# An expert layer whose results are collected with tokens on partitions, on top of the residual, and a final norm that reads them there

## The chip, the cores and the metric

One core of a Trainium2 chip runs the whole program. The metric is the device time of one execution in microseconds: the median of 3 runs, 805.72 us (803.02 to 806.88).

## The reference

A trunk of two layers over 256 tokens of width 1024, all in fp32. Each layer is a mixer and a hierarchical mixture of 16 experts, both behind an RMS norm with a learned shift, scale and gate; a final RMS norm ends it. Cut to the last expert sub-layer and the norm:

```python
hcur = rms_norm(x, norm2_g[layer]) * (1 + sc2) + sh2
for e in range(N_EXPERTS):
    hid = jax.nn.silu(xt @ w_gate[e]) * (xt @ w_up[e])
    y = y + gates[:, e:e + 1] * (hid @ w_down[e])
x = x + g2 * y
return rms_norm(x, final_norm_g)
```

Each token has a gate above zero for two experts only. Widths: 1024 to 512 (gate and up) and 512 to 1024 (down).

## The kernel before, in words

Tensors that lie with features on partitions hold feature n * 8 + k (n the partition, k from 0 to 7) in block k; the residual is `xT`, 128 partitions x 8 blocks x 256 tokens. The tokens of an expert layer are gathered into slots, sorted by expert, and the slots are worked through as 20 tasks of 64 or 32 slots (`_tasks`, lines 66 to 82): 8 tasks of 64 and 12 of 32 a layer. Four (or two) tasks fill a pack of 128 slots; there are 7 packs.

A task is: `first_half` and `second_half` (lines 1473 and 1484: gate and up products, in 2 column groups of TensorE for 64 slots, in 4 for 32 slots), `hidden` (Silu and product), `turn` (transposes), and `project` (line 1493), which calls `down` (line 1381). `down` puts its result with slots on partitions in a PSUM bank; G is 128 / slots, and each of the G column groups makes the part of the features whose k lies in its q = 8 / G blocks. The weights of `down` lie in a buffer of [128, 2048] with features in order n * 8 + k, so its moving operand `src[:, :, q * g:q * (g + 1)]` reads q neighbouring values, then the next n, 8 values further on. `project` then splits the result into a rounded part and a rest (`yp`, lines 1511 and 1512, ScalarE and VectorE, G times each), reordered so that k is outermost. When a pack is full, `combine` (line 1514) adds it to `acc`, four PSUM banks: 16 products of 256 columns, whose moving operand is `ptts`, the 0/1 matrix of slots by tokens, so the sum comes out with features on partitions and tokens in columns. `acc` is started with four zero products (line 1529). All of it runs one task ahead: the halves of task i + 1 stand around the transposes and the `down` of task i (loop at line 1531).

After the last `combine`, eight VectorE steps (line 1563) add gate times `acc` to `xT`. The final norm (lines 1584 to 1630) squares `xT` on ScalarE, sums over features with products against ones (`square_sums`), turns the sums to tokens (`to_tokens`), turns `xT` block by block to tokens on partitions (line 1602; some blocks with a diagonal matrix of the norm's gains, `dg`), takes 1/sqrt as Exp of Ln, scales into `ot` on ScalarE and VectorE, and stores in four transfers of 256 KB.

TensorE and SP (the queue of all loads) run in the order of the program; VectorE and ScalarE do so inside `in_order()`, elsewhere a scheduler orders them. Weights come in pieces of 1 MB in a fixed order (`moe`, line 166: six pieces an expert) into 15 buffers and a few more; SP issues a load as soon as TensorE has emptied a buffer (`pump`, line 261, called from `free`). Which experts the loads fetch is known only after routing, so the stream stops there and starts again. Line 135 is the helper of all products. At task 9 stands a branch for tokens that overflow an expert's slots (`whatever_is_left`, line 1432, with `further` in it); with these inputs it is not taken.

Of the kernel before, what the change touches and what calls it, by code (L numbers as in the profile page):

```python
# [19 lines left out]
P = 128  # L20
# [92 lines left out]
def trunk_kernel(ctx: ExitStack, tc: tile.TileContext, a, out, dbg=None):  # L113
# [20 lines left out]
    def mm(o, l, r, start=False, stop=False):  # L134
        T.matmul(o, l, r, start=start, stop=stop, skip_group_check=True)  # L135
# [1167 lines left out]
    def place(rr, e, base, G):  # L1303

        pe = sb.tile([P, 2, P], BF, name="pe", tag="pt")
# [4 lines left out]
        return pe  # L1310

    def moe_layer(l, before, then):
        table(LEXP)
        if l == 0:
            drain_ada()
# [19 lines left out]
        with in_order():  # L1335
            g3, rr, hs, ofi, exi, pe = route(l, wa, cb, lg, th, tl, sm)

        def load_window(o, base, n, tag=None):
            w = sb.tile([P, KD, n], F32, name="win", tag=tag or "sq", bufs=1 if tag else 3)
            A.copy(w, hs[:, :, ds(o + base, n) if base else ds(o, n)])  # L1340
            return w

        def slots(e, base, pe):
# [8 lines left out]
            ptt = sb.tile([P, S], F32R, name="ptt", tag="rs")  # L1352
            A.copy(ptt, b[:, 0:S])
            return ptt, gs


        def gate_up(w, wts, b, G, halves=(0, 1)):
# [15 lines left out]
        def turn(hid, b, G, tag="ht"):  # L1373
# [3 lines left out]
            ht = sb.tile([P, m, G, P // G], F32, name="ht", tag=tag)  # L1377
            A.copy(ht.rearrange("p c g s -> p (c g s)"), b[:, 0:n])  # L1378
            return ht

        def down(ht, wts, G, bs2=(6,)):

            n, r, m, q = D // G, P // G, DE // G // P, KD // G
            ys = [bank(i) for i in bs2]
            y = [ys[g % len(ys)] for g in range(G)]
            for j in range(4):
                src = k3(wts[j // 2], 2)[:, j % 2, :].rearrange("p (n k) -> p n k", k=KD)
                for g in range(G):
                    mm(y[g][g * r:(g + 1) * r, 0:n], ht[:, j % m, j // m, :], src[:, :, q * g:q * (g + 1)],
                       start=(j == 0), stop=(j == 3))  # L1390
            return y

        def above(e, n):
# [3 lines left out]
        def further(p, base, bk):  # L1397

            def load(name, tag, cut):
                r = sb.tile([P, 2048], F32, name="raw", tag=tag)  # L1400
                e = p if p < FIXED else nc.sync.value_load(exi[0:1, p:p + 1], min_val=0, max_val=NE - 1)
                nc.sync.dma_start(k3(r, 4 if name != "moe_w_down" else 2), cut(a[name][l, e]))
                return r

            tags = ("f8", "m8", "f8", "m8")
            wts = []
            for h in range(2):
                for name in ("moe_w_gate", "moe_w_up"):
                    wts.append(load(name, tags[len(wts)],
                                    lambda w: w.rearrange("(p k) n -> p k n", k=KD)[:, 4 * h:4 * h + 4, :]))  # L1410
                if h == 0:
                    b = bank(bk)
                    pt, gs = slots(p, base, place(rr, p, base, 2))
                    o = nc.scalar.value_load(ofi[0:1, 16 + p:17 + p], min_val=0, max_val=2 * S - base)
                    w = load_window(o, base, 64, "m8b")
                gate_up(w, wts, b, 2, (h,))
            ht = turn(hidden(b, gs, 2, "r8"), b, 2, "m8b")
            wts = [load("moe_w_down", tags[h], lambda w: w.rearrange("(j p) n -> p j n", p=P)[:, 2 * h:2 * h + 2, :])
                   for h in range(2)]
            y = down(ht, wts, 2)[0]  # L1420
            y2 = sb.tile([P, 2, 512], F32R, name="y2", tag="r8")
            A.copy(y2[:, 0, :], y)
            V.tensor_sub(y2[:, 1, :], y, y2[:, 0, :].bitcast(F32))
            for n in range(2):
                yx = y2[:, n, :]
                for kk in range(4):
                    for g in range(2):
                        k, rows = 4 * g + kk, slice(64 * g, 64 * g + 64)
                        mm(acc[k // 2][:, (k % 2) * S:(k % 2 + 1) * S],
                           yx.rearrange("p (n k) -> p k n", k=4)[rows, kk, :], pt[rows, :])  # L1430

        def whatever_is_left(bk):
            left = nc.values_load(ofi[0:1, 32:33], min_val=0, max_val=2 * S)
# [59 lines left out]
        def project(i, ht):  # L1493
            t = TASKS[i]
            p, r, G = t["p"], t["row"], P // t["n"]
            if t["first"]:
                dw_[p] = take_all([("moe_w_down", l, p)] * 2)
            y = down(ht, [w for w, _ in dw_[p]], G, (4 + n % 2, 7) if i == n - 1 else (6,))
            if i == n - 1:
                table(LEXP)  # L1500
            if t["last"]:
# [3 lines left out]
                yy[0] = [sb.tile([P, KD, P], F32R, name="yp", tag=x) for x in ("m4a", "m4b")]  # L1505
            yh, yl = yy[0]
            q, w = KD // G, P // G
            for g in range(G):
                src = y[g][g * w:(g + 1) * w, 0:D // G].rearrange("p (n k) -> p k n", k=q)
                o = slice(r, r + w), slice(q * g, q * (g + 1))  # L1510
# [1 line left out]
                V.tensor_sub(yl[o[0], o[1], :], src, yh[o[0], o[1], :].bitcast(F32))  # L1512

        def combine(j, last=False):
            for x in range(2):
# [5 lines left out]
        yy, ptts = [None], {}  # L1521
# [6 lines left out]
        for a4 in acc:  # L1528
            mm(a4, zero, identb.unsqueeze(1).to_broadcast([P, 4, P]), start=True)
        prepare(1)  # L1530
        for i, t in enumerate(TASKS):
            if i == LEFT:
# [22 lines left out]
                ptts[j] = turned_pack(j)  # L1555
            if st["fin"]:
                ada_flush(7, -1)
        with in_order():
            combine(PACKS - 1, last=True)
            before()  # L1560
            warm(WARM[5])
            for k in (0, 1, 4, 5, 2, 3, 6, 7):
# [15 lines left out]
    dump("x2", xT)  # L1578
    odd_mixer(1)
    dump("x3", xT)  # L1580
    moe_layer(1, lambda: None, lambda: None)
    dump("x4", xT)

    ot = sb.tile([P, 2, D], F32, name="ot", tag="f8")
    ov = ot.rearrange("p t (n k) -> p t k n", k=KD)
    rt = sb.tile([P, 2], F32, name="rt", tag="Rrt")
    fb = sb.tile([P, D], F32, name="fb", tag="r8")
    nc.sync.dma_start(fb, a["final_norm_g"].partition_broadcast(P))
    fv = fb.rearrange("p (n k) -> p k n", k=KD)

    dg = sb.tile([P, 4, P], F32, name="dg", tag="m8b")
    for i, k in enumerate((0, 1, 4, 5)):
        V.tensor_scalar(dg[:, i, :], ident, ng3[:, k:k + 1], None, op0=OP.mult)
    table(LEXP)
    with in_order():
        st2 = bank(0)
        tk = bank(1)
        bk = [bank(4 + i) for i in range(4)]

        def turned(k):  # L1600
            for t in range(2):
                o = bk[k // 2][:, t * S + k % 2 * P:t * S + (k % 2 + 1) * P]
                if k % 4 < 2:
                    mm(o, xT[:, k, t * P:(t + 1) * P], dg[:, k // 4 * 2 + k % 2, :], start=True, stop=True)
                else:
                    T.transpose(o, xT[:, k, t * P:(t + 1) * P], ident)  # L1606

        ks = []
        for _, k in square_sums(st2, 0, 4):
            ks.append(k)  # L1610
            if len(ks) in (3, 5, 7):
                turned(ks[-3])
                turned(ks[-2])
        tk = to_tokens(st2, tk, diag[:, 0:1])
        turned(ks[-2])
        turned(ks[-1])
        A.activation(rt, tk[:, :, 0], AF.Ln, scale=1.0 / D, bias=eps)  # L1617
        A.activation(rt, rt, AF.Exp, scale=-0.5)  # L1618
        for t in range(2):
            for i in range(4):  # L1620
                c = slice(2 * i, 2 * i + 2)
                src = k3(bk[i][:, t * S:(t + 1) * S], 2)
                if i % 2:
                    V.scalar_tensor_tensor(ov[:, t, c, :], src, rt[:, t:t + 1], fv[:, c, :], op0=OP.mult, op1=OP.mult)  # L1624
                else:
                    A.activation(ov[:, t, c, :], src, AF.Copy, scale=rt[:, t:t + 1])
    for tt in range(2):
        for h2 in range(2):
            c = slice(h2 * 512, (h2 + 1) * 512)
            nc.sync.dma_start(out[0, tt * P:(tt + 1) * P, c], ot[:, tt, c])  # L1630


_INS = ["x", "c", "rel_bias", "norm1_g", "norm2_g", "w_ada", "b_ada", "ev_w_in", "ev_w_out",
# [21 lines left out]
```

## Time and profile before

| | us |
|---|---|
| median of 3 runs | 805.72 |
| lowest, highest | 803.02, 806.88 |
| the profiled execution | 803.79 |
| its span in the profile | 802.0 |
| TensorE products busy | 695.3 |
| VectorE, ScalarE busy | 375.4, 236.8 |

Times in the profile are from the start of the span. A row names the line, the operation, the tiles written and read, the shape of one instruction and how many; "PEld" is TensorE's load of a stationary operand, which overlaps its products. An fp32 product appears as two records. The granted clock is 1.00 when TensorE runs at full speed.

### The profile page before, as it was taken

To read this page: it belongs to the slowest core of one execution; us is meant where nothing else is said; L and a number is where in the kernel's file an instruction comes from. 1 tells how busy PE (TensorE), PEld (TensorE's weight loads), DVE (VectorE), ACT (ScalarE), POOL (GpSimd) and SP (SyncE) were. 2 spreads that over 40 slices of the span, in tenths; PEclk is the share of its full clock that TensorE was granted. 3 is DMA by queue.
4 is the path that set the end of the run, shared out by engine and by line. 5 is a ranking of instruction groups with operands and counts; after the bars stand their busy time and mean duration, and the time that the engine had idled before them with its cause. 6 is when DMAs were issued, how large, how long until landed. Compare 5 with 4: busy or idle time off the path is not lost. (4 is left out here: it accounts for less than half of the span.)

```text
span 802.0 us, 18126 instructions
## 1 busy us (share of the span) xinstructions
PE 695.3 (87%) x7589; PEld 478.9 (60%) x7589; DVE 375.4 (47%) x866; ACT 236.8 (30%) x530; POOL 13.2 (2%) x33
## 2 busy tenths in 40 slices
PE   4699899978999959997669989998999995999765
PEld 3376358956666637544338878775666664755433
DVE  2516788877322212211158999997722231221114
ACT  3211143041222213211055326473322221321114
POOL 0010002000000000000000000000000000000000
PEclk9799899999999979999899999999999998999988
DMA  8989999967999999999999999321899999999991
GB/s 300 370 290 402 400 406 409 418 253 300 350 416 412 417 407 407 416 418 415 415 400 397 398 409 409 103 81 54 335 401 415 408 419 392 411 416 413 417 406 66
DMA packets 70029, 288.12 MB, mean 359 GB/s; under 512 B 8909, under 2 KB 11273, under 8 KB 53544
## 3 DMA queue, kind: packets, MB, share of 16 engines
q1 hardware_dynamic: 69928, 286.77, 90.1%
q8 instruction: 63, 1.03, 0.5%
q14 instruction: 38, 0.31, 0.1%
HBM read 285.69 MB, written 1.06 MB: 358 GB/s over the span
## 5 line engine op out<-in xcount | busy, mean ns | idle before, releaser
L135 PE MATMUL b<-raw,win 128*32 128x128 f32 (+1 forms) x3712 | 198.5, 309 | 36.3 <-DVEq L1434 16.9
L135 PEld LDWEIGHTS b<-raw,win 128*32 128x32 f32 (+1 forms) x3712 | 141.2, 120 | 85.7 <-issue 28.9
L1512 DVE TENSOR_TENSOR yp<-b,yp 32x256 fp32r<-32x256 f32 (+1 forms) x128 | 62.5, 488 | 143.5 <-ACT yp L1511 143.3
L135 PE MATMUL b<-raw,ht 128*32 128x256 f32 (+1 forms) x1024 | 113.5, 460 | 15.1 <-DMA raw<-in_moe_w_down_dram 15.0
L1511 ACT CAST yp<-b 32x256 fp32r<-32x256 f32 (+1 forms) x128 | 53.3, 417 | 131.0 <-PE b L135 93.2
L135 PEld LDWEIGHTS b<-raw,ht 128*32 128x32 f32 (+1 forms) x1024 | 42.1, 119 | 69.8 <-issue 34.5
L319 DVE SCALAR_TENSOR_TENSOR raw<-raw,csil 128x1024 f32<-128x1024 f32 x56 | 74.6, 1332 | 4.3 <-DMA raw<-in_w_ada_dram 3.2
L1370 DVE SCALAR_TENSOR_TENSOR hid<-hid,gs,b 128x128 f32<-128x128 f32 (+1 forms) x40 | 16.0, 401 | 113.4 <-ACT hid L1369 113.4
L914 DVE SCALAR_TENSOR_TENSOR ac<-hqk,dw,ac 128x256 f32<-128x256 f32 x120 | 50.7, 481 | 0.3
L135 PE MATMUL b<-h,raw 128*128 128x256 f32 x192 | 44.8, 392 | 5.3 <-ACT h L584 2.9
L135 PE MATMUL b<-hh,whf 128*128 128x256 f32 x160 | 41.7, 299 | 4.1 <-DVE whf L588 3.7
L135 PEld LDWEIGHTS b<-h,raw 128*128 128x128 f32 x192 | 37.1, 196 | 13.1 <-ACT h L584 3.8
L1369 ACT ACTIVATE hid<-b 128x128 f32<-128x128 f32 (+1 forms) x40 | 12.8, 320 | 105.5 <-PE b L135 105.5
L135 PE MATMUL b<-mx,raw 128*128 128x256 f32 x160 | 40.6, 409 | 0.0
L135 PEld LDWEIGHTS b<-mx,raw 128*128 128x128 f32 x160 | 38.8, 335 | 1.0 <-issue 0.8
L135 PE MATMUL b<-hl,whf 128*128 128x256 f32 x128 | 37.2, 290 | 0.4 <-DVE hl L849 0.4
L1378 ACT COPY ht<-b 128x128 f32<-128x128 f32 (+1 forms) x40 | 12.3, 308 | 84.6 <-PE b L1376 84.5
L1471 DVE TENSOR_REDUCE gs<-b 128x1 f32<-128x3 f32 x40 | 6.4, 161 | 65.9 <-PE b L135 65.5
L135 PE MATMUL b<-ptt,yp 128*128 128x256 f32 x224 | 34.4, 295 | 2.4 <-ACT yp L1511 1.6
L135 PEld LDWEIGHTS b<-hh,whf 128*128 128x128 f32 x160 | 29.7, 200 | 7.5 <-DVE whf L588 4.1
L135 PEld LDWEIGHTS b<-ptt,yp 128*128 128x128 f32 x224 | 28.4, 188 | 9.3 <-ACT yp L1511 6.6
L135 PE MATMUL b<-raw,h 128*128 128x512 f32 x64 | 31.5, 640 | 0.0
(287 smaller groups left out, 825.9 us busy)
## 6 DMA issues: line engine op xcount, KB each, us to landing
raw<-in_moe_w_gate_dram SPq DMA_DIRECT2D x64, 1024.0 KB, 13.1
raw<-in_moe_w_up_dram SPq DMA_DIRECT2D x64, 1024.0 KB, 14.7
raw<-in_moe_w_down_dram SPq DMA_DIRECT2D x64, 1024.0 KB, 16.5
raw<-in_w_ada_dram SPq DMA_DIRECT2D x48, 1024.0 KB, 15.8
raw<-in_ev_w_in_dram SPq DMA_DIRECT2D x10, 1024.0 KB, 13.1
raw<-in_od_w_in_dram SPq DMA_DIRECT2D x10, 1024.0 KB, 18.4
raw<-in_ev_w_out_dram SPq DMA_DIRECT2D x4, 1024.0 KB, 15.0
raw<-in_od_w_out_dram SPq DMA_DIRECT2D x4, 1024.0 KB, 14.0
```

The lines of the kernel that those rows point to most:

```text
L135: T.matmul(o, l, r, start=start, stop=stop, skip_group_check=True)
L319: ins = V.scalar_tensor_tensor(acc, src, csil[:, k:k + 1], acc, op0=OP.mult, op1=OP.add)
L914: V.scalar_tensor_tensor(ac[:, m, :], src, dw[:, m, j:j + 1], ac[:, m, :], op0=OP.mult, op1=OP.add)
L1369: A.activation(hid, b[:, 0:n], AF.Silu)
L1370: V.scalar_tensor_tensor(hid, hid, gs, b[:, n:2 * n], op0=OP.mult, op1=OP.mult)
L1378: A.copy(ht.rearrange("p c g s -> p (c g s)"), b[:, 0:n])
L1471: V.tensor_reduce(gates[i], g, AX.X, OP.add)
L1511: A.copy(yh[o[0], o[1], :], src)
L1512: V.tensor_sub(yl[o[0], o[1], :], src, yh[o[0], o[1], :].bitcast(F32))
```

## The change

`moe_layer` takes a new argument `rows`, true for the second layer alone. There, `down` reads its weights so that its columns come out in order k, n. `project` multiplies the result by the gate row (`gains`), splits it in SBUF and stores the parts by blocks. `combine` swaps its operands: the 0/1 matrix is stationary and the results move, 8 products of 512 columns a pack, and the sum has tokens on partitions. `acc` starts from the residual, turned by 16 plain products against the identity. The gate rows are made at the start of the layer: POOL scales eight identity blocks by the gate (`dg`), and TensorE multiplies them with ones, once for 32-slot and once for 64-slot tasks. The final norm reads `acc` directly: squares on ScalarE for the first 128 tokens, statistics on VectorE for the others, and scaling from the banks into `ot`, a quarter of it over ScalarE and POOL; two stores of 512 KB. The table of final gains (`fb`) is loaded at task 17 of 20. In the branch that is not taken the buffers move to other tiles. The core of the diff:

```diff
-        def down(ht, wts, G, bs2=(6,)):
+        def down(ht, wts, G, bs2=(6,), rows=False):
...
-                    mm(y[g][g * r:(g + 1) * r, 0:n], ht[:, j % m, j // m, :], src[:, :, q * g:q * (g + 1)],
-                       start=(j == 0), stop=(j == 3))
+                    c = src[:, :, q * g:q * (g + 1)]
+                    mm(y[g][g * r:(g + 1) * r, 0:n], ht[:, j % m, j // m, :],
+                       c.rearrange("p n k -> p k n") if rows else c, start=(j == 0), stop=(j == 3))
...
+            bs2 = (6,) if i < n - 1 else (4 + n % 2,) if rows else (4 + n % 2, 7)
+            y = down(ht, [w for w, _ in dw_[p]], G, bs2, rows)
...
+            if rows:
+                ys = sb.tile([P, D // G], F32, name="ys", tag="sq", bufs=3)
+                V.tensor_mul(ys, y[0][:, 0:D // G], gains[G])
+                yr = sb.tile([P, D // G], F32R, name="yr", tag="sq", bufs=3)
+                A.copy(yr, ys)
+                ys2 = ys.bitcast(F32R)
+                rest(ys2, ys, yr)
+                for g in range(G):
+                    o = slice(r, r + w), slice(q * g, q * (g + 1))
+                    A.copy(yh[o[0], o[1], :], k3(yr[g * w:(g + 1) * w, :], q))
+                    V.tensor_copy(yl[o[0], o[1], :], k3(ys2[g * w:(g + 1) * w, :], q))
+                return
...
         def combine(j, last=False):
+            if rows:
+                pt = ptts.pop(j)
+                for t in range(2):
+                    for h in range(2):
+                        for x in range(2):
+                            mm(acc[2 * t + h], pt[:, t * P:(t + 1) * P],
+                               yy[0][x][:, 4 * h:4 * h + 4, :], stop=(last and x == 1))
+                return
...
+        if rows:
+            ada_flush(7, -1)
+            dg = [sb.tile([P, 4, P], F32, name="dg", tag="sq", bufs=3) for _ in range(2)]
+            for k in range(KD):
+                G.tensor_scalar(dg[k // 4][:, k % 4, :], ident, M(l, 5, k), None, op0=OP.mult)
...
+        if rows:
+            for n4, tag in ((4, "pt"), (2, "gr2")):
+                b = bank(6)[:, 0:D // n4]
+                for k in range(KD):
+                    g, kk = k * n4 // KD, k % (KD // n4)
+                    w = P // n4
+                    mm(b[g * w:(g + 1) * w, kk * P:(kk + 1) * P], ones[:, 0:w], dg[k // 4][:, k % 4, :],
+                       start=True, stop=True)
+                gains[n4] = sb.tile([P, D // n4], F32, name="gains", tag=tag)
+                A.copy(gains[n4], b)
+            for t in range(2):
+                for k in range(KD):
+                    mm(acc[2 * t + k // 4][:, k % 4 * P:(k % 4 + 1) * P], xT[:, k, t * P:(t + 1) * P], ident, start=(k % 4 == 0))
+        else:
+            for a4 in acc:
+                mm(a4, zero, identb.unsqueeze(1).to_broadcast([P, 4, P]), start=True)
...
+            if rows and i == n - 3:
+                before()
         with in_order():
             combine(PACKS - 1, last=True)
+            if rows:
+                then(acc)
+                return
...
+    def final_norm(acc):
...
+        for h in range(2):
+            sq = sb.tile([P, 512], F32, name="sq", tag="sq", bufs=3)
+            A.activation(sq, acc[h], AF.Square, accum_out=ss[:, h:h + 1])
+        for h in range(2):
+            V.bn_stats(st6[:, h, :], acc[2 + h])
+        V.tensor_add(rt[:, 0:1], ss[:, 0:1], ss[:, 1:2])
+        A.activation(rt[:, 0:1], rt[:, 0:1], AF.Ln, scale=1.0 / D, bias=eps)
+        A.activation(rt[:, 0:1], rt[:, 0:1], AF.Exp, scale=-0.5)
+        V.bn_aggr(mv, st6)
+        V.scalar_tensor_tensor(rt[:, 1:2], mv[:, 0:1], mv[:, 0:1], mv[:, 1:2], op0=OP.mult, op1=OP.add)
+        A.activation(rt[:, 1:2], rt[:, 1:2], AF.Ln, bias=eps)
+        A.activation(rt[:, 1:2], rt[:, 1:2], AF.Exp, scale=-0.5)
+        sq = sb.tile([P, 512], F32, name="sq", tag="sq", bufs=3)
+        A.activation(sq, acc[1], AF.Copy, scale=rt[:, 0:1])
+        G.tensor_mul(ov[:, 0, 4:8, :], k3(sq, 4), fv[0][:, 4:8, :])
+        for x in (0, 2, 3):
+            c = slice(x % 2 * 4, x % 2 * 4 + 4)
+            V.scalar_tensor_tensor(ov[:, x // 2, c, :], k3(acc[x], 4), rt[:, x // 2:x // 2 + 1], fv[0][:, c, :],
+                                   op0=OP.mult, op1=OP.mult)
+        for t in range(2):
+            nc.sync.dma_start(out[0, t * P:(t + 1) * P, :], ot[:, t, :])
```

## Rows read from the trace of the kernel before

**Rows 1.** The page: TensorE's and the other engines' busy time and share.

```profile
PE 695.3 (87%) x7589; PEld 478.9 (60%) x7589; DVE 375.4 (47%) x866; ACT 236.8 (30%) x530; POOL 13.2 (2%) x33
```

**Rows 2.** Windows: us, busy PE, PEld, DVE, ACT, POOL, granted clock, DMA share, GB/s.

```profile
580.00:600.00 20.00, 20.00 (x380) 12.59 (x378) 5.19 (x15) 5.12 (x14) 0.00 (x0) 1.00 1.01 403
...
740.00:760.00 20.00, 14.16 (x204) 8.50 (x201) 2.37 (x5) 2.25 (x6) 0.00 (x0) 1.00 1.02 414
760.00:780.00 20.00, 13.70 (x186) 7.10 (x186) 2.15 (x5) 2.33 (x6) 0.00 (x0) 0.83 1.02 415
```

**Rows 3.** Waits of TensorE's products, 560 to 802 us: total us, times, longest.

```profile
PE b L135 <- DMA raw<-in_moe_w_down_dram: 7.7, 8, 1.4
PE b L135 <- DMA raw<-in_moe_w_up_dram: 5.0, 7, 1.3
PE b L135 <- DMA raw<-in_moe_w_gate_dram: 3.1, 4, 1.8
```

**Rows 4.** Groups of instructions, whole span: busy us, mean ns of one, idle before.

```profile
L135 PEld LDWEIGHTS b<-h,raw 128*128 128x128 f32 x192 | 37.1, 196 | 13.1 <-ACT h L584 3.8
...
L135 PEld LDWEIGHTS b<-mx,raw 128*128 128x128 f32 x160 | 38.8, 335 | 1.0 <-issue 0.8
...
L677 ACT CAST who<-raw 128x256 fp32r<-128x256 f32 x12 | 8.1, 683 | 6.7 <-PE b L135 6.7
...
L977 ACT CAST mhl<-g 128x256 fp32r<-128x256 f32 x4 | 1.5, 405 | 0.0
```

**Rows 5.** Order of time: two runs of stationary loads, start us, us, count.

```profile
162.74 3.91 PEld L135 LDWEIGHTS b<-mx,raw 128*128 128x128 f32 x16 [0.41 <-issue]
...
789.45 0.97 PEld L135 LDWEIGHTS b<-dg,xT 128*128 128x128 f32 x8 [0.41 <-issue]
```

**Rows 6.** Order of time: products of expert tasks and a combine.

```profile
611.38 3.65 PE L135 MATMUL b<-raw,ht 128*64 128x512 f32 x16
...
617.17 1.92 PE L135 MATMUL b<-raw,win 128*32 128x128 f32 x64
618.92 2.01 PE L135 MATMUL b<-raw,ht 128*32 128x256 f32 x32
...
625.03 3.65 PE L135 MATMUL b<-raw,win 128*64 128x256 f32 x32
...
632.33 2.80 PE L135 MATMUL b<-ptt,yp 128*128 128x256 f32 x16
...
759.96 5.35 PE L135 MATMUL b<-raw,ht 128*64 128x512 f32 x16 [1.45 <-DMA raw<-in_moe_w_down_dram]
```

**Rows 7.** Order of time: the zero products and the next loads that SP issues.

```profile
580.42 1.04 PE L135 MATMUL b<-identb,zero 128*128 128x512 bf16 x4
...
582.53 1.26 SPq L252 DMA_DIRECT2D raw<-in_moe_w_down_dram  x2
```

**Rows 8.** Groups of instructions: a product on POOL, statistics on VectorE.

```profile
L548 POOL TENSOR_TENSOR x<-x,ju 128x512 f32<-128x512 f32 x1 | 1.8, 1842 | 24.3 <-ACT x L546 24.3
...
L717 DVE BATCH_NORM_STATS2 st<-m8b 128x6 f32<-128x512 f32 x2 | 1.3, 686 | 0.0
```

**Rows 9.** Order of time: the end of the kernel.

```profile
783.24 1.49 PE L135 MATMUL b<-raw,ht 128*32 128x256 f32 x16 [0.52 <-DMA raw<-in_moe_w_down_dram]
...
784.78 1.66 ACT L1511 CAST yp<-b 32x256 fp32r<-32x256 f32 x4 [1.42 <-PE b L135]
...
786.04 1.92 PE L135 MATMUL b<-ptt,yp 128*128 128x256 f32 x14 [0.34 <-ACT yp L1511]
...
787.30 3.23 DVE L1563 SCALAR_TENSOR_TENSOR xT<-b,mod,xT 128x256 f32<-128x256 f32 x8 [0.34 <-PE b L135]
...
795.12 0.26 ACT L1617 ACTIVATE rt<-b,eps 128x2 f32<-128x2 f32 x1 [0.70 <-PE b L135]
...
795.65 2.40 DVE L1624 SCALAR_TENSOR_TENSOR ot<-b,rt,fb 128x256 f32<-128x256 f32 x4 [5.12 <-ACT rt L1618]
...
796.97 1.99 SPq L1630 DMA_DIRECT2D out_dram<-ot  x4
```

More of the change, by code (lines that the diff above doesn't have):

```diff
@@ L1301, in place_pack, with place @@
         return pe
-    def place(rr, e, base, G):
-        pe = sb.tile([P, 2, P], BF, name="pe", tag="pt")
+    def place(pe, rr, e, base, G):
         for t in range(2):
@@ L1309, in place, with moe_layer @@
                             rr[:, t, e:e + 1], float(-base), op0=OP.subtract, op1=OP.is_equal)
-        return pe
-    def moe_layer(l, before, then):
+    def moe_layer(l, before, then, rows=False):
         table(LEXP)
@@ L1336, in moe_layer, with load_window, slots @@
             g3, rr, hs, ofi, exi, pe = route(l, wa, cb, lg, th, tl, sm)
-        def load_window(o, base, n, tag=None):
-            w = sb.tile([P, KD, n], F32, name="win", tag=tag or "sq", bufs=1 if tag else 3)
+        def load_window(o, base, n):
+            w = sb.tile([P, KD, n], F32, name="win", tag="sq", bufs=3)
             A.copy(w, hs[:, :, ds(o + base, n) if base else ds(o, n)])
             return w
-        def slots(e, base, pe):
+        def slots(e, base, pe, ptt):
             b = bankbf(7)
@@ L1351, in slots @@
             V.tensor_reduce(gs, g, AX.X, OP.add)
-            ptt = sb.tile([P, S], F32R, name="ptt", tag="rs")
             A.copy(ptt, b[:, 0:S])
-            return ptt, gs
+            return gs
         def gate_up(w, wts, b, G, halves=(0, 1)):
@@ L1371, in hidden, with turn @@
             return hid
-        def turn(hid, b, G, tag="ht"):
+        def turn(hid, b, G, ht=None):
             n, m = DE // G, DE // G // P
@@ L1412, in further @@
                     b = bank(bk)
-                    pt, gs = slots(p, base, place(rr, p, base, 2))
+                    room = sb.tile([P, 2048], F32, name="room", tag="m8b")
+                    pe = room[:, 0:P].bitcast(BF).rearrange("p (t n) -> p t n", t=2)
+                    pt = sb.tile([P, S], F32R, name="ptt", tag="rs")
+                    place(pe, rr, p, base, 2)
+                    gs = slots(p, base, pe, pt)
                     o = nc.scalar.value_load(ofi[0:1, 16 + p:17 + p], min_val=0, max_val=2 * S - base)
-                    w = load_window(o, base, 64, "m8b")
+                    w = k3(room[:, 512:1024])
+                    A.copy(w, hs[:, :, ds(o + base, 64) if base else ds(o, 64)])
                 gate_up(w, wts, b, 2, (h,))
-            ht = turn(hidden(b, gs, 2, "r8"), b, 2, "m8b")
+            ht = turn(hidden(b, gs, 2, "r8"), b, 2, room[:, 1024:1024 + S])
             wts = [load("moe_w_down", tags[h], lambda w: w.rearrange("(j p) n -> p j n", p=P)[:, 2 * h:2 * h + 2, :])
                    for h in range(2)]
-            y = down(ht, wts, 2)[0]
+            y = down(ht, wts, 2, rows=rows)[0]
             y2 = sb.tile([P, 2, 512], F32R, name="y2", tag="r8")
+            if rows:
+                ys = k3(room[:, 1536:], 1)[:, 0, :]
+                V.tensor_mul(ys, y, gains[2])
+                y = ys
             A.copy(y2[:, 0, :], y)
@@ L1425, in further @@
                 yx = y2[:, n, :]
+                if rows:
+                    for g in range(2):
+                        c = slice(64 * g, 64 * g + 64)
+                        for x in range(2):
+                            mm(acc[2 * x + g], pt[c, x * P:(x + 1) * P], yx[c, :])
+                    continue
                 for kk in range(4):
                     for g in range(2):
-                        k, rows = 4 * g + kk, slice(64 * g, 64 * g + 64)
+                        k, c = 4 * g + kk, slice(64 * g, 64 * g + 64)
                         mm(acc[k // 2][:, (k % 2) * S:(k % 2 + 1) * S],
-                           yx.rearrange("p (n k) -> p k n", k=4)[rows, kk, :], pt[rows, :])
+                           yx.rearrange("p (n k) -> p k n", k=4)[c, kk, :], pt[c, :])
         def whatever_is_left(bk):
@@ L1527, in moe_layer @@
         acc = [bank(i) for i in range(4)]
-        for a4 in acc:
-            mm(a4, zero, identb.unsqueeze(1).to_broadcast([P, 4, P]), start=True)
+        if rows:
+            for n4, tag in ((4, "pt"), (2, "gr2")):
[13 more added lines that the diff above has]
+                mm(a4, zero, identb.unsqueeze(1).to_broadcast([P, 4, P]), start=True)
         prepare(1)
@@ L1580, in trunk_kernel @@
     dump("x3", xT)
[L1581 to L1618, printed above, removed]
-        for t in range(2):
[L1620 to L1630, printed above, removed]
+    fv = []
+    def final_gains():
+        fb = sb.tile([P, D], F32, name="fb", tag="r8")
+        nc.sync.dma_start(fb, a["final_norm_g"].partition_broadcast(P))
+        fv.append(fb.rearrange("p (n k) -> p k n", k=KD))
+    def final_norm(acc):
+        ot = sb.tile([P, 2, D], F32, name="ot", tag="f8")
+        ov = ot.rearrange("p t (n k) -> p t k n", k=KD)
+        ss = sb.tile([P, 2], F32, name="ss", tag="Rm1")
+        rt = sb.tile([P, 2], F32, name="rt", tag="Rrt")
+        st6 = sb.tile([P, 2, 6], F32, name="st6", tag="st6")
+        mv = sb.tile([P, 2], F32, name="mv2", tag="rs2")
+        for h in range(2):
[17 more added lines that the diff above has]
+                                   op0=OP.mult, op1=OP.mult)
+        for t in range(2):
+            nc.sync.dma_start(out[0, t * P:(t + 1) * P, :], ot[:, t, :])
@@ L1633 @@
+    moe_layer(1, final_gains, final_norm, rows=True)
 _INS = ["x", "c", "rel_bias", "norm1_g", "norm2_g", "w_ada", "b_ada", "ev_w_in", "ev_w_out",
```

9 lines of the change are left out of this document (6 added, 3 removed).

## The prediction

> **What bounds the kernel now.** I read the page's busy shares first, then stage windows of the last layer, then who waited for whom there, then the order of time at its start and end. Of the span TensorE is busy 87% [rows 1]; that is an average. The stage that the change touches is the second expert layer. In 580 to 600 us TensorE is busy for the whole window while the loads already run at 403 GB/s; in 740 to 760 and 760 to 780 it is busy 14.16 and 13.70 us of 20 and the loads hold 414 and 415 GB/s [rows 2]. So the stage has two limits in turn: TensorE sets the pace first, the weight stream later, and the two are close. How close: TensorE's product queue waits for weights 7.7 + 5.0 + 3.1 = 15.8 us from 560 us on [rows 3]. Less than 16 us more of TensorE work in this stage hides behind the loads; any more moves the end.
>
> **The down products.** This is the term that decides. Now a `down` reads from each weight row runs of 2 or 4 neighbouring fp32 values in every 8 (k innermost). After it, with `"p n k -> p k n"`, it reads one value, jumps 32 bytes, reads the next. The count of products and columns is the same, so the only question is what such a read costs. The present runs cost nothing: a 64-slot down (16 records of 512 columns, 8,192 columns) takes 3.65 us, and a gate-and-up half with 8,192 columns from contiguous rows 3.65 us as well; for 32 slots it is 2.01 against 1.92 us [rows 6]. No row shows a moving operand at a 32-byte step, so I bound it. Lower end: 0 (the runs of two show no penalty, and no reason for a gain is in sight). Upper end: rows in which another read has exactly this step. The output projection of the first layer loads its stationary operand from the same kind of tile with this step: 335 ns a load, against 196 ns where the columns are contiguous [rows 4]. In a run of such loads that is 3.91 / 16 = 0.244 us each against 0.97 / 8 = 0.121 us [rows 5]: 0.123 us more for 128 values, 0.96 ns a value. ScalarE pays the same: its cast of 128x256 values at this step takes 683 ns, a contiguous one 405 ns [rows 4], which is 1.09 ns a value. I take 0.96 ns, since the weight load is the nearest row: same engine, same memory, same step. A 64-slot down runs two column groups side by side, each of 8 records x 512 = 4,096 columns: + 3.9 us. A 32-slot down has four groups of 2,048 columns: + 2.0 us. The layer has 8 and 12 of them: 8 x 3.9 + 12 x 2.0 = 55 us more on TensorE, twice the present time of the downs. With ScalarE's figure it would be 63 us.
>
> The Trainium skill, in "Advanced Engine Details and Errata", section "SBUF Cachelines", has a rule that speaks against this edit: SBUF lines are 16 bytes, and a read wants at least two hits in a line to run at full rate, otherwise there is a penalty. By that rule the present runs (two or four values in a line) are free and the new ones (one value) are not; it gives no price. The trace agrees as far as it goes: free at two values, 335 against 196 ns at one.
>
> **The block of preparation.** Behind the first expert's second half the change puts on TensorE 16 products for the gains and 16 plain products that turn the residual, and takes out four zero products (1.04 us, rows 7). Each fp32 product of 128 columns is two records at about 0.121 us [rows 5]. The 16 turns are 32 x 0.121 = 3.9 us; the gains, if nothing overlapped, the same, but four or two column groups overlap in part, so 3.2; between the two gain sets the bank must be copied out, 0.5. Together 3.9 + 3.2 + 0.5 - 1.0 = + 6.6, say 7 us. The scaled diagonals come from POOL: a 128x512 product there took 1.84 us [rows 8], so eight of 128 columns some 8 x 0.46 = 3.7 us, beside the first expert's products; if that cover is short, up to 3.7 us more. Everything queued behind this block on TensorE is late by as much, and so are the loads that SP issues when TensorE has emptied a buffer, the first at 582.53 us [rows 7].
>
> **Combines and collecting.** A combine is 8 products of 512 columns in place of 16 of 256: same columns. Now one takes 2.80 us [rows 6] where it waits for the last casts; the same product in the tail runs at 1.92 / 14 = 0.137 us, 16 of them 2.2 us [rows 9]. The new collecting reads the product bank once and splits from SBUF, so I take 0.5 us off each of six: - 3 us (ends: 0 and - 4). DVE and ScalarE get two or three more steps of some 0.4 us a task; they lie beside the next expert's half, 1.92 or 3.65 us [rows 6], and matter only in the last task. The window copies now share three buffers with the collecting and must follow the second half; the next down, 2 us or more, covers a copy of 256 or 512 columns. The table of final gains moves up in the program, but the last weight loads are already ahead of it on SP's queue: 0. The code in the branch for overfull experts does not run: 0.
>
> **What the load stream gives back.** If TensorE sets the pace to the end, its 15.8 us of waits vanish [rows 3], and so does work at a reduced clock: a 64-slot down of 3.65 us takes 5.35 at 759.96 us [rows 6], with 0.83 granted in that window [rows 2]; - 2 us. Shift of the last down product: 55 + 7 - 3 - 16 - 2 = + 41 us.
>
> **The tail.** Now the last product (from 783.24 us) is followed by casts, combine, eight residual steps of 3.23 us, squares, turning, Ln and Exp, and two engines' 2.40 us of scaling [rows 9]; from the last cast's start at 784.78 us to the span's end at 802.0 it is 17.2 us. After: gain, cast, rest and four copies at some 0.42 us each [the casts in rows 9], 2.9; the five products of the combine that still wait, 5 x 0.27 = 1.4; one statistics step of 512 columns, 0.69 [rows 8]; sum, Ln and Exp 0.8 (twice 0.26 and the handovers, rows 9); three scalings of 512 columns in DVE's row, 3 x 1.15 = 3.5, a little under twice the 2.40 / 4 for 256 [rows 9]; aggregate steps 0.3; then from the last scaling (795.65 + 2.40 = 798.05) to the end as now, 3.95, and 0.4 for fewer and bigger stores. Sum 13.9: - 3.3 us (ends - 2 and - 5; POOL's quarter at 1.84 us and more [rows 8] must not be the last).
>
> **Sum.** + 41 - 3.3 = + 37.7 us. The profiled execution took 803.79 us (span 802.0 and 1.8 around it): 841.5. It lies 1.9 us under the median of the runs, 805.72, so for the median I say 843 us. A difference under 0.5%, 4 us, can't be told from none here.
>
> **Rivals.**
> 1. *The single reads hide* (not slower by what can be measured). Point that decides: whether the array takes columns slowly enough for one value in 32 bytes. For it: runs of two lose nothing, and each column group takes a column only every 0.9 ns (3.65 us / 4,096). Then TensorE has only the 7 us block more. Its lateness reaches SP at 582.53, and the loads, which keep above 400 GB/s almost throughout, can't catch up what they lose; I take 5 us, less 3.3 in the tail: 807.4 us. Against it: three readers in the rows pay.
> 2. *As 1, and the loads' lead also swallows the block* (faster). Then only the tail counts: - 3.3, 802.4 us; with a tail of - 5, 800.7. For it: 15.8 us of waits lie later in the stage. Against it: SP issues only as TensorE frees buffers.
> 3. *Half a penalty*, because two records read each value and line reads overlap: 27 us; 27 + 7 - 3 - 16 - 2 - 3.3 = + 9.7, 815 us.
>
> **Chances.** Forecast 0.58, rival 1 0.22, rival 2 0.12, rival 3 0.08. Slower by over 0.5%: 0.58, 0.06 of rival 3 and 0.07 of rival 1 (its loads lose the full 7 us and POOL is late): 0.71. Same: 0.13 + 0.02 + 0.04 = 0.19. Faster: 0.02 + 0.08 = 0.10. The forecast's own range is 826 to 852 (a down at 1.7 times its time, up to ScalarE's price). The whole range leaves out rival 2 and the edges: 805 to 850.
>
> **What would show it.** Right: a 64-slot down of over 6 us and a 32-slot down near 4 us at full clock; TensorE's waits for weights gone; load rate of the layer below 400 GB/s. Wrong: downs still at 3.65 and 2.01 us; then the time from the last load's landing to the end (802.0 - 783.24 = 18.8 us now) and a gap in the loads just behind the issue that is now at 582.53 us tell rivals 1 and 2 apart.

## The result and the profile after

The changed kernel takes 834.35 us (median of 4 runs, 833.78 to 834.97) against 806.04 us for the kernel before in the same comparison: 1.036 times as long, 95% interval 1.033 to 1.040. Forecast were 843 us, range 805 to 850, slower with a chance of 0.71. The profiled execution took 833.78 us, its span 832.0.

The page's row of busy times answers to [rows 1], and the windows of the second expert layer to [rows 2] (us, then busy time of each engine, granted clock, DMA share, GB/s):

```profile
PE 736.5 (89%) x7545; PEld 476.7 (57%) x7545; DVE 384.6 (46%) x898; ACT 247.2 (30%) x549; POOL 19.6 (2%) x42
```

```profile
600.00:620.00 20.00, 20.00 (x312) 11.37 (x307) 6.13 (x19) 6.82 (x17) 0.00 (x0) 1.00 0.71 266
...
760.00:780.00 20.00, 20.00 (x126) 9.41 (x124) 5.09 (x10) 5.87 (x11) 0.00 (x0) 1.00 1.02 419
```

Early in the layer the loads fall to 266 GB/s while TensorE is busy without a pause; late, loads and TensorE are both full, where TensorE had 6 us in 20 to spare before. The waits of TensorE's products from 560 us on (total, times, longest) answer to [rows 3]: not one for weights is left.

```profile
PE b L135 <- ACTq L1450: 5.8, 1, 5.8
...
PE b L135 <- ACT yp L1535: 2.0, 2, 1.8
...
PE b L135 <- ACT gains L1581: 1.2, 1, 1.2
```

In order of time: the block of preparation, the first down, a 32-slot down, the last down and the tail (start, us). They answer to [rows 6, 7, 9].

```profile
580.70 0.66 PE L135 MATMUL b<-dg,ones 128*32 128x128 f32 x16
...
582.61 1.58 PE L135 MATMUL b<-dg,ones 128*64 128x128 f32 x16 [1.25 <-ACT gains L1581]
...
584.12 3.84 PE L135 MATMUL b<-cst,xT 128*128 128x128 f32 x32
...
589.03 1.26 SPq L252 DMA_DIRECT2D raw<-in_moe_w_down_dram  x2
...
592.06 7.55 PE L135 MATMUL b<-raw,ht 128*64 128x512 f32 x16
...
705.13 3.64 PE L135 MATMUL b<-raw,win 128*32 128x128 f32 x64 [5.85 <-ACTq L1450]
...
711.68 3.86 PE L135 MATMUL b<-raw,ht 128*32 128x256 f32 x32
...
814.48 3.88 PE L135 MATMUL b<-raw,ht 128*32 128x256 f32 x32 [0.35 <-ACT ht L1378]
...
820.18 2.49 PE L135 MATMUL b<-yp,ptt 128*128 128x512 f32 x8 [1.82 <-ACT yp L1535]
...
824.34 3.21 DVE L1677 SCALAR_TENSOR_TENSOR ot<-b,rt,fb 128x512 f32<-128x512 f32 x3 [0.23 <-ACT rt L1667]
...
825.38 1.52 POOL L1674 TENSOR_TENSOR ot<-sq,fb 128x512 f32<-128x512 f32 x1 [248.54 <-ACT sq L1673]
```

A 64-slot down takes 7.55 us instead of 3.65, a 32-slot down 3.86 instead of 2.01 [rows 6].

**Where the 30 us lie.** I cut the span at four points that all kernels here have: the start of the first down, the start of the first down behind the branch of task 9, the end of the last down, the end of the span. Behind the branch TensorE's next products wait 5.8 us; before, 8.3. The first down, the products behind the branch and the first down there, in the kernel before:

```profile
585.56 3.65 PE L135 MATMUL b<-raw,ht 128*64 128x512 f32 x16
...
674.91 3.57 PE L135 MATMUL b<-raw,win 128*32 128x128 f32 x64 [8.26 <-DVEq L1434]
...
680.48 2.01 PE L135 MATMUL b<-raw,ht 128*32 128x256 f32 x32
```

The last down ends at 784.73 us before (783.24 + 1.49) and at 818.36 after (814.48 + 3.88).

| us | before | after | difference |
|---|---|---|---|
| start of the span to the first down | 585.56 | 592.06 | + 6.5 |
| stretch 1, to the first down behind the branch | 94.92 | 119.62 | + 24.7 |
| stretch 2, to the end of the last down | 104.25 | 106.68 | + 2.4 |
| tail | 17.27 | 13.64 | - 3.6 |

Sum + 30.0 = 832.0 - 802.0. Each stretch holds four downs of 64 and six of 32 slots, so the same 4 x 3.9 + 6 x 1.85 = 26.7 us of new work. In front of the branch nearly all of it lengthens the program; behind it almost none. That was not in the prediction: it had read two limits in turn from [rows 2], but made one sum for the layer. The experiments take it up.

### The profile page after: what moved, and what is told of

It reads as the page before. It is cut to its first block, busy times and chain, and to the rows that moved or that the text cites. A ratio compares the mean times of both kernels' runs of the same rounds, so it can differ in the third digit from the quotient of the medians.

```text
span 832.0 us, 18094 instructions
## 1 busy us (share of the span) xinstructions
PE 736.5 (89%) x7545; PEld 476.7 (57%) x7545; DVE 384.6 (46%) x898; ACT 247.2 (30%) x549; POOL 19.6 (2%) x42
## 5 line engine op out<-in xcount | busy, mean ns | idle before, releaser
L135 PE MATMUL b<-raw,win 128*32 128x128 f32 (+1 forms) x3712 | 196.1, 308 | 24.9 <-DVEq L1450 8.4
L135 PE MATMUL b<-raw,ht 128*32 128x256 f32 (+1 forms) x1024 | 162.8, 605 | 7.9 <-DMA raw<-in_moe_w_down_dram 6.8
L1542 DVE TENSOR_TENSOR yp<-b,yp 32x256 fp32r<-32x256 f32 (+1 forms) x64 | 31.2, 488 | 69.1 <-ACT yp L1541 69.0
L1528 DVE TENSOR_TENSOR ys<-b,gains 128x256 f32<-128x256 f32 (+1 forms) x20 | 10.6, 532 | 86.8 <-PE b L135 86.8
L1541 ACT CAST yp<-b 32x256 fp32r<-32x256 f32 (+1 forms) x64 | 26.7, 417 | 64.8 <-PE b L135 46.0
L1530 ACT CAST yr<-ys 128x256 fp32r<-128x256 f32 (+1 forms) x20 | 9.8, 490 | 75.6 <-DVE ys L1528 75.5
## 6 DMA issues: line engine op xcount, KB each, us to landing
raw<-in_w_ada_dram SPq DMA_DIRECT2D x48, 1024.0 KB, 15.8
```

Source lines behind the costliest of these rows:

```text
L1528: V.tensor_mul(ys, y[0][:, 0:D // G], gains[G])
L1530: A.copy(yr, ys)
L1541: A.copy(yh[o[0], o[1], :], src)
```

## Experiments

**1. The single reads by themselves** (`single_alone`): the kernel before, with the new order of reading in the second layer's downs and the reordering in `project` dropped to match; no gains, no turned residual, old tail.

```diff
+        def single(G):
+            return l == 1
...
+                    c = src[:, :, q * g:q * (g + 1)]
                     mm(y[g][g * r:(g + 1) * r, 0:n], ht[:, j % m, j // m, :],
-                       src[:, :, q * g:q * (g + 1)], start=(j == 0), stop=(j == 3))
+                       c.rearrange("p n k -> p k n") if single(G) else c, start=(j == 0), stop=(j == 3))
```

> The kernel before with one part of the change: the second layer's down reads single values at a 32-byte step, everything else is as before. Theory A (the single reads double the downs, and TensorE then sets the pace to the end): the 64-slot down takes about 7.5 us and the 32-slot down about 3.9 us, TensorE no longer waits for weights, and the time is 832 to 836 us, 26 to 30 us over before. Theory B (the loss came from the block at the start of the layer, the new collecting or the shared buffers, and the longer downs hide behind the loads): 803 to 810 us.

Measured 831.16 us against 805.19 (1.029, 1.023 to 1.034): + 26.0. Downs of 7.54 and 3.86 us, no wait for weights. Theory A holds, with a time 0.8 us under its range.

**2. Everything but the single reads** (`runs_back`): the changed kernel with downs that read runs again; VectorE reorders in the multiplication by the gains.

```diff
-                       c.rearrange("p n k -> p k n") if rows else c, start=(j == 0), stop=(j == 3))
+                       c, start=(j == 0), stop=(j == 3))
...
-                V.tensor_mul(ys, y[0][:, 0:D // G], gains[G])
+                V.tensor_mul(k3(ys, q), y[0][:, 0:D // G].rearrange("p (n k) -> p k n", k=q), k3(gains[G], q))
```

> The changed kernel with the downs' reads as before (runs of 2 or 4 values); VectorE puts the result into block order when it multiplies by the gain. Theory A: downs back at 3.65 and 2.01 us, and what is left is the block at the start (6.5 us later on TensorE) against the shorter tail (3.6 us): 803 to 809 us; 807 if the loads pass the block's delay on, 802 if their lead swallows it. Theory B: 825 us or more.

Measured 808.59 us (1.0036, 1.0005 to 1.0067): + 3.4. The two parts add up: 26.0 + 3.4 = 29.4 against the 28.3 measured for the whole. Waits for weights are back (7.5 + 6.3 + 3.2 us), and the multiplication takes as long with the reordering as without (692 and 425 ns in both kernels). From the second half of task 0 (576.82 us before, 580.30 here) to the end of the last down (784.73 and 794.14) it is 5.9 us longer. To the first down alone it is 6.2 us longer (8.74 and 14.98), so almost all of what the block adds is passed on; the tail is 2.6 us shorter. The tail gains less than in the changed kernel, since its combine runs slower (2.49 us there):

```profile
793.01 1.13 PE L135 MATMUL b<-raw,ht 128*32 128x256 f32 x16 [1.29 <-DMA raw<-in_moe_w_down_dram]
795.96 3.63 PE L135 MATMUL b<-yp,ptt 128*128 128x512 f32 x8 [1.82 <-ACT yp L1535]
```

**3. The block made shorter** (`late_residual`): the second kernel, with the residual turned and added at task 16, zero products at the start again, and the two gain sets in two banks.

```diff
+            if rows and i == 16:
+                residual()
...
-                b = bank(6)[:, 0:D // n4]
+                b = bank(6 if n4 == 4 else 7)[:, 0:D // n4]
```

> As the changed kernel with reads in runs, but the residual's 16 turning products are added to the banks at task 16 of 20, where TensorE waits for weights, on top of four zero products at the start, and the two gain sets use two banks, so that the second need not wait for the first one's copy. About 5 us of the block leave the start. If the loads pass the block's delay on: 3 to 5 us under the kernel with reads in runs, about 802 to 804. If their lead swallows the delay: the same as that kernel within 1 us.

Measured 806.98 us (1.0001, 0.997 to 1.003), and 806.82 in a second comparison of 12 runs (`late_again`, 1.001). That is 1.6 us less than in experiment 2: not the 3 to 5 expected, nor the same within 1 us. With runs from 803 to 810 us I take it for the right direction and no more. The gains now take 2.18 us and the zero products 1.04, so that the block adds 2.1 us instead of 6.2. But from the second half of task 0 to the end of the last down it is still 213.1 and 211.9 us (in the two profiles), against 213.8 in experiment 2: of the 4.1 us taken off, 0.7 and 1.9 came back. Where the rest went was not tested.

**4. What a moving operand costs by its step** (`probe_steps`): the kernel before, with seven groups of 8 unread fp32 products behind its end, one line of code each.

```diff
+    for i in range(8):
+        T.matmul(pb, ones, xf.rearrange("p (n s) -> p s n", s=8)[:, 0, 0:256], start=True, stop=True, skip_group_check=True)
```

> The kernel before, with fp32 products behind its end that nobody reads, 8 of each kind: the same stationary ones, 256 moving columns read from one tile at steps of 1, 2, 4 and 8 values, in runs of 2 and of 4 in every 8, and in runs of 2 that straddle a 16-byte boundary (values 3 and 4 of each 8). Their times alone are of interest. If the cost is by 16-byte lines with fewer than two reads: steps 1 and 2 and both aligned runs take 0.21 us a record, steps 4 and 8 about 0.43, and the straddling runs 0.43 too. If it is by the length of a run: step 2 is slow as well, and straddling runs are as quick as aligned ones. If it is by the step in bytes: the times grow from step to step.

The groups of instructions (busy us, mean ns), by line: 1636 neighbours, 1638 step of 2 values, 1640 step of 4, 1642 step of 8, 1644 runs of two in eight, 1646 runs of four, 1648 runs of two that begin at value 3, across a 16-byte border:

```profile
L1642 PE MATMUL b<-xT,ones 128*128 128x256 f32 x16 | 7.6, 642 | 0.0
L1640 PE MATMUL b<-xT,ones 128*128 128x256 f32 x16 | 7.4, 631 | 0.0
L1648 PE MATMUL b<-xT,ones 128*128 128x256 f32 x16 | 7.4, 631 | 0.0
L1644 PE MATMUL b<-xT,ones 128*128 128x256 f32 x16 | 3.9, 393 | 0.0
L1638 PE MATMUL b<-xT,ones 128*128 128x256 f32 x16 | 3.8, 388 | 0.0
L1636 PE MATMUL b<-xT,ones 128*128 128x256 f32 x16 | 3.6, 379 | 0.0
L1646 PE MATMUL b<-xT,ones 128*128 128x256 f32 x16 | 3.6, 379 | 0.0
```

This is one execution; the granted clock is 1.00 in every window from 795 us to its end. Records overlap, so the busy time over 16 is the price of one: 0.475 us at a step of 8 and 0.225 for neighbours, that is (7.6 - 3.6) / 16 / 256 = 0.98 ns a value more. Runs of two inside a 16-byte border are nearly free (3.9 against 3.6 us for 16 records), across it they cost as much as a step of 4 values (7.4), and a step of two (still two values in 16 bytes) is nearly free too (3.8). The Trainium skill's rule, in "Advanced Engine Details and Errata", section "SBUF Cachelines", says just this: two hits in a 16-byte line, or a penalty. The trace agrees in all seven cases and adds the price.

**5. Only the 32-slot downs, only the 64-slot downs** (`single_32`, `single_64`): as experiment 1, with

```diff
-            return l == 1
+            return l == 1 and G == 4
```

and G == 2. The question is how much of the work hides, and whether it matters where it lies.

> The kernel before, with single reads in the twelve 32-slot downs of the second layer alone: 12 x 1.85 = 22 us more work on TensorE, ten of the twelve downs before 710 us. Theory A, a pool: whatever TensorE has to spare in the layer (15.8 us of waits for weights, and about 10 us of branch stall and reduced clock, 27 us in all as the kernel with all reads single gave back) is used up first, wherever the work lies. Then 22 us hide: 804 to 808 us. Theory B, the lead: extra work hides only as long as the loads have buffers to run ahead into. Early in the layer they have few, so SP issues later for each delay there, the stream falls under 400 GB/s before 700 us, and later, where the stream sets the pace, the loss shows: 812 to 820 us, with waits for weights left in the last 60 us.

> The kernel before, with single reads in the eight 64-slot downs of the second layer alone: 8 x 3.9 = 31 us more work on TensorE, 16 us of it before 670 us and 16 us after 715 us, where the products wait for weights. Theory A, a pool of 27 us: 807 to 811 us. Theory B, the lead: the late 16 us hide in the waits, the early 16 us delay the stream: 810 to 818 us, and less than the kernel with 22 us in the 32-slot downs, although there is more work.

Measured 819.72 us (1.0175, 1.013 to 1.022) and 821.05 us (1.0176, 1.013 to 1.022): + 14.4 and + 15.7 against 805.36. The pool of 27 us is refuted: of 22 us of work, 14 do not hide. Theory B is right for the 32 slots; for the 64 slots it is 3 us too low, and that more work would cost less did not come. Nor was I right about what is lost later: the time behind the branch did not grow. The first down behind the branch and the last half down (a wait for weights cuts this down into two runs of 16 records), first of the 32-slot kernel, then of the 64-slot kernel:

```profile
692.54 3.86 PE L135 MATMUL b<-raw,ht 128*32 128x256 f32 x32
...
794.57 2.02 PE L135 MATMUL b<-raw,ht 128*32 128x256 f32 x16 [0.39 <-DMA raw<-in_moe_w_down_dram]
```

```profile
697.83 2.02 PE L135 MATMUL b<-raw,ht 128*32 128x256 f32 x32
...
800.50 1.52 PE L135 MATMUL b<-raw,ht 128*32 128x256 f32 x16 [0.43 <-DMA raw<-in_moe_w_down_dram]
```

Stretch 2 is 104.05 and 104.19 us, with 11.1 and 15.6 us more work in it, against 104.25 before. With first downs at 586.07 and 589.15 us, stretch 1 is 106.47 and 108.68 us against 94.92: + 11.6 for 11.1 us of work, + 13.8 for 15.6. A new theory follows: two stretches, of which the first passes all on and the second hides some 24 us.

**6. The same work in front of the branch and behind it** (`single_early`, `single_late`): as experiment 1, with single reads in tasks 0 to 9 or in tasks 10 to 19 alone (`project` passes its i).

```diff
-            return l == 1
+            return l == 1 and i >= 10
```

> The kernel before, with single reads only in the downs of tasks 10 to 19 of the second layer, behind the branch: four of 64 and six of 32 slots, 4 x 3.9 + 6 x 1.85 = 26.7 us more work on TensorE. Theory of two stretches: behind the branch the stream sets the pace, and 24 us of extra work go into the waits for weights and into work that ran at a reduced clock; 2 to 3 us are passed on: 806 to 810 us, and the time from the first down behind the branch to the end of the last one grows from 104.3 to 106 to 107 us. Theory of one pool, or of a share (half of any added work is passed on, wherever it lies): 816 to 820 us.

> The kernel before, with single reads only in the downs of tasks 0 to 9 of the second layer, in front of the branch: again four of 64 and six of 32 slots, the same 26.7 us. Theory of two stretches: TensorE sets the pace there, so all is passed on but some 2 to 3 us of the 8.3 us that TensorE waits at the branch; the stream loses as much and has no reserve behind: 827 to 831 us, with waits for weights still some 12 to 16 us in the last 100 us. Theory of one pool, or of a share: the same as the kernel with the late downs, 816 to 820 us.

Measured 805.56 us behind the branch (1.0003, 0.997 to 1.004) and 827.69 us in front of it (1.029, 1.023 to 1.035), against 805.22. Equal work on TensorE, + 22.5 us in front and nothing that can be measured behind (the interval is - 2.5 to + 2.9 us): place decides, and pool and share are refuted. The late kernel has no wait for weights left and took 0.4 us less than its range; the early one still has 7.8 + 5.6 + 2.3 us of them, as expected. The first down, the first behind the branch and the last, of the late kernel and then of the early one:

```profile
585.38 3.65 PE L135 MATMUL b<-raw,ht 128*64 128x512 f32 x16
...
681.04 3.86 PE L135 MATMUL b<-raw,ht 128*32 128x256 f32 x32
...
783.66 3.88 PE L135 MATMUL b<-raw,ht 128*32 128x256 f32 x32 [0.52 <-ACT ht L1378]
```

```profile
583.31 7.54 PE L135 MATMUL b<-raw,ht 128*64 128x512 f32 x16
...
702.31 2.01 PE L135 MATMUL b<-raw,ht 128*32 128x256 f32 x32
...
804.93 1.54 PE L135 MATMUL b<-raw,ht 128*32 128x256 f32 x16 [0.49 <-DMA raw<-in_moe_w_down_dram]
```

All kernels cut the same way, from such rows (new work in brackets; in experiment 1 the rows stand at 586.75, 705.59 and 808.25 + 3.88 us):

| us | stretch 1 | stretch 2 | tail |
|---|---|---|---|
| before | 94.92 | 104.25 | 17.3 |
| 32-slot downs | 106.47 (11.1) | 104.05 (11.1) | 17.3 |
| 64-slot downs | 108.68 (15.6) | 104.19 (15.6) | 17.3 |
| late | 95.66 (0) | 106.50 (26.7) | 17.3 |
| early | 119.00 (26.7) | 104.16 (0) | 17.3 |
| all downs | 118.84 (26.7) | 106.54 (26.7) | 17.3 |
| the changed kernel | 119.62 (26.7) | 106.68 (26.7) | 13.6 |

Stretch 2 stays at 104.1 to 104.2 us with up to 15.6 us of new work, and grows by 2.3 to 2.4 with 26.7: it has room for some 24 us. Stretch 1 has room for none but 2 to 3 us at the branch.

Why the two differ is seen at SP's queue in the kernel before. These are its waits (total us, times, longest), from 585 to 680 us and then from 680 to 783 us:

```profile
SPq L252 <- PE b L135: 57.0, 25, 8.2
```

```profile
SPq L252 <- DMA raw<-in_moe_w_up_dram: 19.0, 10, 2.0
SPq L252 <- DMA raw<-in_moe_w_gate_dram: 17.8, 9, 2.5
SPq L252 <- DMA raw<-in_moe_w_down_dram: 17.5, 10, 2.3
SPq L252 <- PE b L135: 4.5, 8, 1.5
```

In stretch 1 SP waits for TensorE to empty buffers, so a slower TensorE slows the loads: in the early kernel they run at 310 to 374 GB/s from 580 to 680 us, against 395 to 418 before. In stretch 2 SP waits for the transfers themselves, and in the late kernel the loads keep 406 to 417 GB/s from 680 to 780 us in spite of the new work.

**7. The clock in the tail** (`warm_end`): the kernel of experiment 3 with unread zero products where TensorE waits in the last three tasks.

```diff
+                if rows and i >= n - 3:
+                    warm(5, bank(6))
                 second_half(i + 1)
+            if rows and i >= n - 3:
+                warm(4)
...
             project(i, ht)
+            if rows and i >= n - 3:
+                warm(5 if i == n - 1 else 2)
```

> The kernel with reads in runs and the late residual, with unread zero products (bf16, 512 columns) behind the halves and downs of the last three tasks, where TensorE waits for weights. Theory: the last downs (1.93 us each) and the last combine (3.78 us) of that kernel run at the lower clock level because TensorE idles between loads; kept busy, they take 1.1 and 2.5 us or less, so the end comes about 2 us earlier: 804 to 805.5 us, 1 to 2.5 us under the kernel without them. Rival: the added products stand in front of products whose weights have landed, or the clock doesn't rise: 806 to 809 us, with the combine still over 3 us.

> The kernel with reads in runs and the late residual once more, on the same chip as the kernel with added zero products, so that the two can be compared: 804 to 808 us, ratio to the kernel before 0.997 to 1.003.

Measured 806.43 us (0.9994, 0.996 to 1.003) with and 806.82 without the zero products, 12 runs each. The last half down and the last combine, with and then without them:

```profile
790.83 1.13 PE L135 MATMUL b<-raw,ht 128*32 128x256 f32 x16 [1.72 <-DMA raw<-in_moe_w_down_dram]
...
793.79 2.49 PE L135 MATMUL b<-yp,ptt 128*128 128x512 f32 x8 [0.64 <-ACT yp L1535]
```

```profile
787.73 1.93 PE L135 MATMUL b<-raw,ht 128*32 128x256 f32 x16 [0.49 <-DMA raw<-in_moe_w_down_dram]
791.49 3.78 PE L135 MATMUL b<-yp,ptt 128*128 128x512 f32 x8 [1.83 <-ACT yp L1535]
```

In its place the theory is right: the granted clock from 785 to 795 us is 1.00 against 0.50 (the lower of its two levels), and from the start of the last half down to the end of the span it is 14.8 us (805.6 - 790.83) against 16.8 (804.5 - 787.73). In the whole, 2 us can't be told with runs that lie up to 8 us apart. 806.43 is outside the 804 to 805.5 expected and inside the rival's 806 to 809, but the rival's sign, a combine of over 3 us, did not come. In these two profiles, it is 225.6 us with and 226.8 without from the second half of task 0 to the end of the span; the stages ahead of it, equal in both, were 2.2 us longer with. No version here is faster than the kernel before by what can be measured.

## Why the prediction was right, and where its sum was off

**The price of the single reads: right.** 3.9 us for a 64-slot down was forecast and measured (7.55 - 3.65); 2.0 and 1.85 for 32 slots. The sum is 53 us against 55. The bound that carried over was the nearest row, TensorE's own weight load with the same step (0.96 ns a value, [rows 4, 5]); the probe gives 0.98. Rivals 1, 2 and 3 fall with it: the reads are not hidden by the array, nor at half price.

**The block: right.** + 6.2 us against 7, from the second half of task 0 (576.82 us before, 577.09 after) to the first down. The + 6.5 of the table also holds what the stages ahead differ by from one execution to the next: kernels that are equal up to there (before, experiments 1, 5 and 6) start their first down between 583.31 and 589.15 us. The gains cost less (0.66 + 1.58), the copy between them more (1.25). POOL was in time: its eight steps took 627 ns each, more than the 0.46 I had taken, but ended before TensorE came to them. SP's next loads go out at 589.03 us instead of 582.53 [rows 7]. That the block's lateness is passed on was right by experiment 2; how much of it a shorter block gives back, experiment 3 leaves open.

**Combines: off.** - 3 us was forecast; all combines together went from 17.5 to 16.4 us of busy time, and the last one waits 1.8 us for its casts.

**The tail: right.** - 3.6 us against - 3.3 (13.64 and 13.9). POOL's quarter took 1.52 us and ended at 826.90, before VectorE's third scaling at 827.55.

**What the load stream gives back: the step that failed in size.** I counted 15.8 us of waits and 2 us of reduced clock, 18 us in all. It was 26: 53.4 us of new work made the two stretches only 27.1 us longer (24.7 + 2.4), and the last down moved by + 33.6 us, not + 41. The groups of TensorE's products in stretch 2 show what I left out (busy us, mean ns, idle before them); first the kernel before, then the changed one:

```profile
L135 PE MATMUL b<-raw,win 128*64 128x256 f32 x256 | 30.0, 383 | 2.2 <-DMA raw<-in_moe_w_up_dram 1.5 <-DMA raw<-in_moe_w_gate_dram 0.7
L135 PE MATMUL b<-raw,win 128*32 128x128 f32 x524 | 18.6, 287 | 7.0 <-DMA raw<-in_moe_w_up_dram 3.5 <-DMA raw<-in_moe_w_gate_dram 2.4 <-issue 1.1
L135 PE MATMUL b<-raw,ht 128*64 128x512 f32 x64 | 16.6, 656 | 3.4 <-DMA raw<-in_moe_w_down_dram 3.4
L135 PE MATMUL b<-raw,ht 128*32 128x256 f32 x192 | 13.9, 422 | 4.3 <-DMA raw<-in_moe_w_down_dram 4.3
```

```profile
L135 PE MATMUL b<-raw,ht 128*64 128x512 f32 x64 | 30.1, 1096 | 0.0
L135 PE MATMUL b<-raw,win 128*64 128x256 f32 x256 | 29.3, 381 | 0.0
L135 PE MATMUL b<-raw,ht 128*32 128x256 f32 x192 | 23.2, 639 | 0.4 <-ACT ht L1378 0.4
L135 PE MATMUL b<-raw,win 128*32 128x128 f32 x524 | 16.0, 273 | 0.0
```

Idle time falls from 16.9 to 0.4 us, close to what I had. But gate and up lose 3.3 us of busy time without any edit, and the downs grow by 22.8 us (13.5 + 9.3) instead of 26.7, which is 3.9 more: 7 us, where I had 2, priced from one down [rows 6] and not from the groups. The kernel before shows two parts of it:

```profile
721.92 1.95 PE L135 MATMUL b<-raw,win 128*64 128x256 f32 x16 [0.44 <-DMA raw<-in_moe_w_up_dram]
...
726.20 3.65 PE L135 MATMUL b<-raw,win 128*64 128x256 f32 x32
...
775.68 1.12 PE L135 MATMUL b<-raw,ht 128*32 128x256 f32 x16 [1.20 <-DMA raw<-in_moe_w_down_dram]
...
780.79 1.94 PE L135 MATMUL b<-raw,ht 128*32 128x256 f32 x16 [1.25 <-DMA raw<-in_moe_w_down_dram]
```

Some 4 us are the clock. In stretch 2 it is granted at 1.00 up to 760 us, and at 0.66 on average from 760 to 765, 770 to 775 and 780 to 785 us, where TensorE has waited for weights between its products. The half down at 780.79 takes 1.94 us there instead of 1.12; together with the down at 759.96 [rows 6] and three more rows it is 4.1 us. The other 3 us are products that a wait cuts in two: 32 records take 3.65 us in one run, and 2 x 1.95 us in two. In the changed kernel nothing waits for weights, and the granted clock is 1.00 from 720 to 800 us. Idle time, clock and cut runs are 24 us together, the room that experiment 6 finds. The remaining 2.5 us are at the branch, where the wait shrinks from 8.3 to 5.8. It shrinks where the 64-slot down in front of it is longer (5.5 to 6.4 us) and not where the 32-slot downs alone are (8.7); that this down runs beside what the branch waits for is read from these numbers, not tested.

**Why one sum still served.** The forecast set off all the new work against all of the layer's waits, which is the pool that experiments 5 and 6 refute. It came out near, and inside its own 826 to 852 us, by luck: half of the work happened to lie in stretch 2, and this half, 26.7 us, just fills the room there. Had the downs been single in the first ten tasks only, the same rule would have hidden 18 of 27 us where 2.6 (by stretch 1) to 4.2 (by the medians) are hidden. In the kernel before, all but 0.7 us of the waits of [rows 3] lie behind 729 us; the same view, cut by stretch, would have shown it. The sign that the loads would run below 400 GB/s held in stretch 1 (266 to 401) and not behind 720 us (415 to 419).

## What to carry to other kernels

Look for a row in which another read has the step that an edit brings in: its price per value, 0.96 ns, held here for another operand: 0.98 in the probe, 0.95 and 0.90 in the downs of 64 and of 32 slots. Cut a stage where the limit changes hands (SP's waits show where), and set new work against the spare time of its own stretch; waits that lie later don't pay for work that lies earlier. Where a reordering must be somewhere, try it in a VectorE step that reads PSUM anyway: here its multiplications took no longer, while in TensorE's moving operand it cost 26 us.

## What was not expected of the hardware

- A step of two fp32 values costs a moving operand next to nothing (388 against 379 ns a record), and runs of two across a 16-byte border cost as much as a step of 4 (631).
- More work sped up other work: with no idle time left, products that nobody had edited took 3.3 us less in stretch 2: 1.2 us of it at a granted clock of 1.00 in place of 0.66 (770 to 775 us), the rest because no wait cut them in two.
- In a tail that waits for loads the clock falls to 0.50 and a combine takes 3.78 us; 5 zero products in front of it, and others in the waits before, kept it at 2.49.
